# Softmax weights scaled in place before they are turned, instead of a factor tile after the product with the values

## The chip, the cores and the metric

The kernel runs on one core of one Trainium2 chip. A core has a matrix engine (TensorE, PE in the profile; its weight loads are PEld), VectorE (DVE), ScalarE (ACT), GpSimd (POOL) and SyncE (SP, which here only issues transfers). Each engine works through its own queue in order, and waits on semaphores for the others. The metric is the device time of one execution in microseconds (us); lower is better.

## The reference

One step of a one-layer hybrid decoder for two groups of tokens that share the weights: a prompt of 512 tokens and a sample group of 8 sequences with 8 new tokens each and 2048 tokens of cached past. A token row is normed and modulated, projected to queries, keys, values and gates, and goes through two attentions in parallel: a forgetting attention (8 heads, 2 key/value heads) and a native sparse attention (8 heads in 2 groups) with three branches, compressed, selected and window. Their outputs are projected, merged by gates, and a squared-ReLU MLP follows. The change touches only the prompt's attention:

```python
def fox_attend(q, cq, q_pos, k, v, ck, k_pos):
    s = einsum('btgrd,bsgd->bgrts', q, k) * HEAD_DIM ** -0.5
    p = masked_softmax(s + cq[:, None] - ck[None, :], k_pos <= q_pos)
    return einsum('bgrts,bsgd->btgrd', p, v)

def nsa_attend(...):
    p_c = masked_softmax(s_compressed, dc >= 0)
    o_c = einsum('bgrtn,bngd->btgrd', p_c, vc)
    ...
    return gates[..., 0:1] * o_c + gates[..., 1:2] * o_s + gates[..., 2:3] * o_w
```

With 512 tokens there are 8 blocks of 64 and 16 are selected, so in the prompt the selected branch reads all earlier tokens, as the window branch does; the compressed branch reads 31 compressed rows. `masked_softmax` divides the exponentials by their sum; the three branches are weighted by a gate per token, head and branch.

## The kernel before

The program has one stage after another: the sample group's compressed keys with the conditioning, the projections, the prompt's attention, the sample group's attention, the merge and output projection, the MLP. The prompt's attention lies between about 288 and 424 us of the profiled span.

It runs in 12 steps (`prompt_attention`, the loop over `steps`): a step is one branch and one head index `r`, for both groups `g` (two heads). Their order is selected 0, 1, window 0, 1, selected 2, 3, window 2, 3, then forgetting 0 to 3 (`slc`, `win`, `fox` in the names). In a step, for each group and each of the four blocks of 128 query tokens (`scores`): PE multiplies the stacked query with the key's high and low parts into a bank of PSUM; DVE subtracts the bias row and takes the row's minimum in one instruction (line 1302, tile `S`); ACT takes the exponential in place and its sum into `den`. Block `i` needs 128(i+1) columns, so a group's tile `S` has 1280 columns, and there are four such tiles. In the selected steps PE also makes the compressed scores (`cs`), and `cmp_heads` makes their softmax, already scaled by gate over sum.

The sum and the gate enter late. `scale` (line 1308) takes the reciprocal of `den`, multiplies it by the gate (not in the forgetting branch), and POOL spreads it over 64 columns per head into a tile `f` of 128x512. One step later `turn_over` (line 1318) transposes the unscaled exponentials on PE in pieces and copies them to the tiles `PT`, mostly on ACT; `factors` (line 1334) transposes `f` on PE, and ACT copies it to `F`. Another step later `weigh` (line 1343) multiplies the turned exponentials with the values into one bank (`o`), with two further products of the compressed branch into another bank (`oc`), and DVE multiplies `o` by `F` and adds.

Banks: four rotate for scores, factors and small products (`mmb`), two for transposes (`trb`), two for accumulators (`accb`: `cs`, `o`, `oc`, and the turned keys and queries).

Beside these steps others run on the same engines: the conditioning's chunks (`ada`, a product and two transposes per step, weights loaded through SP), POOL's bias rows (`bias_rows`, line 1270) and copies of the key stacks (line 1249), the sample group's selection (`sample_compare`, `sample_rank`, DVE), and from step 9 the sample group's tables (`sample_tables`, line 1556, POOL).

The order of the instructions on each engine is made by a planner that simulates a timeline with costs of its own; `link` (line 93) lets `weigh` and the first turn follow a given PE instruction by hand, and `issue_after` holds the sample group's side work behind the last minimum of its step.

## Time and profile before

| what | value |
|---|---|
| median of 3 runs | 1143.32 us (1142.42 to 1147.64) |
| the profiled execution's own time | 1140.26 us |
| its span (first to last instruction) | 1138.6 us |
| PE busy in the span | 1114.6 us, 98% |
| DVE busy | 763.3 us, 67% |
| ACT busy | 576.9 us, 51% |
| POOL busy | 316.0 us, 28% |
| granted PE clock | full |

A row of a group reads: line of the kernel, engine, operation, written tile <- read tiles, shape written <- shape read, count, then busy time in us, mean ns of one, and the idle time of the engine just before with what ended it. Tile names leave out numbers: `Sslc` is the score tile of any selected step. A piece of a chain reads: start in us, length, engine, tile, line, count. A row of waits reads: engine, tile and line that waited, what released it, us in total, times, longest.

### The profile page before, as it was taken

The page shows a single profiled execution, that of the slowest core. Times are in us where ns is not written, and L with a number is a line of the kernel's source. Part 1 is how long each engine was busy: PE and PEld are TensorE (multiplying, and loading weights), DVE is VectorE, ACT ScalarE, POOL GpSimd, SP SyncE. Part 2 cuts the span into 40 slices and gives each one's busy share as a digit, 9 for nine tenths or more (in the row PEclk, how much of TensorE's full clock was granted, in tenths as well). Part 3 has the DMA queues.
Part 4 walks back from the last instruction along what each step waited for, and adds up shares of the span by engine and source line. Part 5 has one row for each costly group of instructions (what it writes and reads, how often), then busy time and mean ns, then how long its engine had stood idle before and what let it go on. Part 6 is the DMA issues. An engine that isn't in the chain of part 4 may idle for free.

```text
span 1138.6 us, 25281 instructions
## 1 busy us (share of the span) xinstructions
PE 1114.6 (98%) x9530; PEld 968.2 (85%) x9530; DVE 763.3 (67%) x1812; ACT 576.9 (51%) x1101; POOL 316.0 (28%) x395
## 2 busy tenths in 40 slices
PE   8999999999999999999999999999999999999998
PEld 5997889999666666777999999889999998888887
DVE  3556586586798856666654446668767654898686
ACT  1465453443877774555433323356566655565420
POOL 4414320000321170001766672002564511101000
PEclk9999999999999999999999999999999999999999
DMA  9998455796586588999999986356454637877732
GB/s 232 244 279 245 132 157 203 251 329 208 179 280 203 176 298 287 309 306 298 241 268 299 317 270 224 107 159 193 152 156 137 195 116 262 312 262 256 244 104 83
DMA packets 188188, 255.52 MB, mean 224 GB/s; under 512 B 23161, under 2 KB 144706, under 8 KB 185890
## 3 DMA queue, kind: packets, MB, share of 16 engines
q1 hardware_dynamic: 148770, 173.03, 49.1%
q0 software_dynamic: 21296, 67.38, 18.3%
q10 hardware_dynamic: 18000, 13.50, 4.0%
q8 instruction: 75, 1.23, 0.4%
q14 instruction: 47, 0.39, 0.1%
HBM read 217.64 MB, written 57.12 MB: 241 GB/s over the span
## 4 chain that ended last, share of the span: by engine, by line
PE 82%; DVE 7%; DMA 6%; SPq 2%; ACT 2%; issue 2%; ACTq 0%; DVEq 0%
PE dn L83 14%; PE mg L83 9%; PE z L83 6%; PE br L83 4%; PE wo L83 4%; PE up L83 3%; DMA cpg<-in_cache_nsa_kv 3%; PE hid L83 3%; PE k L89 3%; PE ss L83 2%; DMA winr<-in_w_in 2%; PE so L83 2%; PE dns L83 2%; SPq L168 2%; PE ct L89 2%
## 5 line engine op out<-in xcount | busy, mean ns | idle before, releaser
L83 PE MATMUL z<-winh,h 128*128 128x264 f32 (+1 forms) x576 | 110.0, 286 | 1.3 <-ACT kcT L118 0.9
L83 PEld LDWEIGHTS z<-winh,h 128*128 128x128 f32 x576 | 91.4, 190 | 3.0 <-ACT kcT L118 1.3
L83 PE MATMUL z<-winl,h 128*128 128x264 f32 (+1 forms) x320 | 88.0, 284 | 0.4 <-DVE winl L137 0.4
L83 PE MATMUL mg<-hH,wmh 128*128 128x288 f32 x240 | 70.5, 295 | 0.0
L83 PE MATMUL mg<-hH,wml 128*128 128x288 f32 x240 | 70.2, 294 | 0.0
L83 PE MATMUL mg<-hL,wmh 128*128 128x288 f32 x240 | 68.4, 295 | 0.0
L83 PE MATMUL hid<-x,w1raw 128*128 128x128 f32 (+1 forms) x384 | 64.2, 310 | 0.2 <-ACT x L118 0.2
L83 PEld LDWEIGHTS z<-winl,h 128*128 128x128 f32 x320 | 60.6, 190 | 0.6 <-DVE winl L137 0.6
L118 ACT ACTIVATE x<-ct 128x512 f32<-128x512 f32 x64 | 36.4, 595 | 46.1 <-PE ct L89 31.8
L83 PEld LDWEIGHTS hid<-x,w1raw 128*128 128x128 f32 x384 | 54.2, 191 | 3.0 <-ACT x L118 0.5
L137 DVE TENSOR_TENSOR wml<-wmr,wmh 128x1024 fp32r<-128x1024 f32 x14 | 20.6, 1473 | 38.8 <-ACT wmh L118 38.8
L83 PEld LDWEIGHTS mg<-hH,wmh 128*128 128x128 f32 x240 | 45.1, 188 | 0.1
L83 PEld LDWEIGHTS mg<-hH,wml 128*128 128x128 f32 x240 | 45.0, 188 | 0.0
L83 PEld LDWEIGHTS mg<-hL,wmh 128*128 128x128 f32 x240 | 44.3, 188 | 0.0
L137 DVE TENSOR_TENSOR wp<-sums,wp 128x1024 fp32r<-128x1024 f32 x26 | 36.6, 1412 | 9.8 <-ACT wp L118 9.3
L137 DVE TENSOR_TENSOR wp<-pu,wp 128x512 fp32r<-128x512 f32 (+1 forms) x26 | 30.9, 1193 | 18.1 <-ACT wp L118 18.1
L2099 POOL TENSOR_TENSOR td<-td 128x512 f32<-128x512 f32 x24 | 34.9, 1457 | 19.4 <-DMA td<-in_w_down 19.2
L118 ACT ACTIVATE u<-u 128x1152 f32<-128x1152 f32 x29 | 33.6, 1160 | 11.7 <-DVE u L106 11.1
L89 PE MATMUL ct<-identF,ro 128*128 128x128 f32 x256 | 36.2, 275 | 3.2 <-DVE ro L121 3.2
L2099 POOL TENSOR_TENSOR td<-td,td 128x512 f32<-128x512 f32 x24 | 33.9, 1412 | 16.1 <-DMA td<-in_w_down 15.4
L118 ACT ACTIVATE mgt<-mg 128x288 f32<-128x288 f32 x32 | 12.5, 408 | 50.3 <-PE mg L83 50.3
L83 PE MATMUL br<-oL,wbh 128*128 128x288 f32 x128 | 37.8, 295 | 0.0
(1182 smaller groups left out, 3584.0 us busy)
## 6 DMA issues: line engine op xcount, KB each, us to landing
adw<-in_w_ada SPq DMA_DIRECT2D x16, 1024.0 KB
foxD<-in_cache_fox_kv SPq DMA_DIRECT2D x128, 128.0 KB
rows<-in_cache_nsa_kv SPq DMA_DIRECT2D x128, 128.0 KB
rows<-foxD SPq DMA_DIRECT2D x26, 512.0 KB
pu<-in_w_up SPq DMA_DIRECT2D x26, 512.0 KB
wdr<-in_w_down SPq DMA_DIRECT2D x26, 512.0 KB
cpg<-in_cache_nsa_kv SPq DMA_DIRECT2D x96, 128.0 KB
td<-in_w_down POOLq DMA_DIRECT2D x24, 512.0 KB, 6.5
```

Source lines behind the costliest of these rows:

```text
L83: ins = self.nc.tensor.matmul(out, a, b, start=start, stop=stop, skip_group_check=True)
L89: ins = self.nc.tensor.transpose(out, in_, self.identF[:n, :n])
L118: return self.nc.scalar.activation(out, in_, f, **kw)
L137: self.splits.append((eng or self.nc.vector).tensor_tensor(l, x, h.bitcast(F32), op=OP.subtract).ins)
L168: self.issued[eng] = getattr(self.nc, eng).dma_start(out, in_).ins
L2099: self.nc.gpsimd.tensor_tensor(out, x, y, op=OP.subtract)
```

## The change

The weights are normalised before they are turned. `scale` is called for each group as soon as that group's scores are issued: DVE takes the reciprocal of the group's four sums, and the four blocks of the tile `S` are multiplied in place by it (and by the gate, as a second per-row scalar, in the selected and window branches). Group 0 does this on POOL, group 1 on DVE. The tile `f`, its transposes and the tile `F` are gone, and so is the multiplication of the result.

The compressed values are written as a 128x128 block-diagonal matrix (zeros elsewhere), and the turned compressed weights get zeros in rows 64 to 127, so that one product with all 128 rows adds both groups' compressed results into the bank `o`. The selected result is copied out by ACT, the window result is added by DVE from the bank, the forgetting result is copied out by DVE.

`den` is laid out by group, the hand-set order of `weigh` starts from the last score product (`scored`) instead of the last product, and the scratch tag `ev` has one buffer instead of five.

```diff
--- before.py
+++ after.py
@@ -1006,7 +1006,8 @@
 
         nc = self.nc
         self.khc = pk.tile([P, 2, 2, 32], F32R, name="khc")
-        self.pvc = pk.tile([64, P], F32, name="pvc")
+        self.pvc = pk.tile([P, P], F32, name="pvc")
+        nc.gpsimd.memset(self.pvc, 0.0)
         self.pxT = []
         for kv in range(2):
             tb = self.trb(f"pct{kv}")
@@ -1075,7 +1076,8 @@
         vb = self.mmb("pvcb")
         for e in range(2):
             self.mm(vb[32 * e:32 * e + 32, 0:P], self.identF[:32, :32], self.pvs, True, True)
-        self.cp(self.pvc, vb[:64, 0:P])
+        for e in range(2):
+            self.cp(self.pvc[32 * e:32 * e + 32, 64 * e:64 * e + 64], vb[32 * e:32 * e + 32, 64 * e:64 * e + 64])
 
 
     OFF = [0, 128, 384, 768, 1280]
@@ -1085,7 +1087,7 @@
 
         self.kpos = pn.tile([P, SEQ], F32, name="kpos")
         self.iota(self.kpos, [[1, SEQ]], base=P - SEQ)
-        late = pn.tile([P, SEQ], F32, tag="ev", bufs=5, name="late")
+        late = pn.tile([P, SEQ], F32, tag="ev", bufs=1, name="late")
         self.ts(late, self.kpos, self.prow, NEG, OP.is_gt, OP.mult)
         self.tt(self.kpos, self.kpos, late, OP.add)
         rows = {("nsa", r): self.bias_rows(pp, r) for r in range(2)}
@@ -1097,6 +1099,7 @@
         self.iota(cneg, [[P, 4], [-16, 32]], base=-31, mult=1)
         gp.tensor_scalar(cneg, cneg, 0.0, NEG, op0=OP.is_lt, op1=OP.mult)
         self.tt(self.cpos, self.cpos, cneg, OP.add)
+        gp.memset(cm[64:128, 1280:1792], 0.0)
 
         kst = {"slc": self.kslc}
         qs = {("nsa", 0): self.qnsa}
@@ -1106,7 +1109,7 @@
         for n, (br, r) in enumerate(steps + [(None, None)] * 2):
             back = []
             if prev:
-                pE, pF, pbr, pr, pw = prev
+                pE, pbr, pr, pw = prev
                 T = [[], []]
 
                 def turn(g, *ks):
@@ -1120,13 +1123,14 @@
                     self.cpb = self.accb(f"cs{r}")
                 kind = "fox" if br == "fox" else "nsa"
                 q, row = qs[kind, rp], rows[kind, r]
-                den = self.small.tile([P, 4, 2], F32, tag="den", bufs=3, name=f"den{br}{r}")
+                den = self.small.tile([P, 2, 4], F32, tag="den", bufs=3, name=f"den{br}{r}")
                 tiles = [self.scores(pp, br, r, g, q[g, e], kst[br][g], row[g], den) for g in range(2)]
                 for i in range(4):
                     tiles[0][1](i)
+                self.scale(br, r, 0, tiles[0][0], den)
             if held:
-                self.chain = self.last_mm.name if br else ""
-                self.weigh(pn, *held)
+                self.chain = self.scored if br else ""
+                self.weigh(*held)
                 held = None
                 for f in back[:1]:
                     f()
@@ -1142,9 +1146,8 @@
                         self.chain = self.last_tr.name
                     tiles[1][1](i)
                     self.chain = None
-                F, cw = self.scale(pn, br, r, den), None
-                if br == "slc":
-                    cw = self.cmp_heads(pn, r)
+                self.scale(br, r, 1, tiles[1][0], den)
+                cw = self.cmp_heads(pn, r) if br == "slc" else None
             for f in back[2:]:
                 f()
             if br:
@@ -1152,13 +1155,11 @@
             if br:
                 self.ada_later()
             if prev:
-                pf = self.factors(pn, f"{pbr}{pr}", pF)
-            if prev:
-                held = pbr, pr, T, pf, pw
+                held = pbr, pr, T, pw
             prev = None
             if br is None:
                 continue
-            prev = ([t[0] for t in tiles], F, br, r, cw)
+            prev = ([t[0] for t in tiles], br, r, cw)
             if n == 0:
                 kst["win"] = self.kstack(self.pr, "win", C_WK)
                 self.oT = self.keep.tile([P, 8, NT], F32, tag="r1", bufs=1, name="oT")
@@ -1295,25 +1296,28 @@
             self.mm(pb[:, 0:n], q[:, P * i:P * i + P], kl[:, 0:n], False, br != "fox")
             if br == "fox":
                 self.mm(pb[:, n - P:n], self.identB, self.diagB, False, True)
+            self.scored = self.last_mm.name
             if br == "slc":
                 self.mm(self.cpb[:, 256 * g + 64 * i:256 * g + 64 * i + 64], q[:, P * i:P * i + P],
                         self.khc[:, g].rearrange("p a n -> p (a n)"), True, True)
 
             self.last_min = nc.vector.tensor_tensor_reduce(S, pb[:, 0:n], row[:, 0:n] if br == "fox" else row[:, SEQ - n:SEQ],
                                                            -1.0, -LOW, OP.add, OP.min, nm[:, i:i + 1]).ins
-            self.last_soft = self.act(S, S, AF.Exp, bias=nm[:, i:i + 1], scale=-1.0, accum_out=den[:, i, g:g + 1]).ins
+            self.last_soft = self.act(S, S, AF.Exp, bias=nm[:, i:i + 1], scale=-1.0, accum_out=den[:, g, i:i + 1]).ins
 
         return E, tile
 
-    def scale(self, pn, br, r, den):
-
-        self.nc.vector.reciprocal(den, den)
-        if br != "fox":
-            c = 3 * r + (1 if br == "slc" else 2)
-            self.tt(den, den, self.gate[:, 0:4, c:c + 13:12], OP.mult)
-        f = pn.tile([P, SEQ], F32, tag="ev", bufs=5, name=f"f{br}{r}")
-        self.nc.gpsimd.tensor_copy(f.rearrange("p (i g d) -> p i g d", i=4, g=2), den[:, :, :, None].to_broadcast([P, 4, 2, 64]))
-        return f
+    def scale(self, br, r, g, E, den):
+
+        self.nc.vector.reciprocal(den[:, g], den[:, g])
+        c = 12 * g + 3 * r + (1 if br == "slc" else 2)
+        eng = self.nc.vector if g else self.nc.gpsimd
+        for i in range(4):
+            S = E[:, self.OFF[i]:self.OFF[i + 1]]
+            if br == "fox":
+                eng.tensor_scalar(S, S, den[:, g, i:i + 1], None, op0=OP.mult)
+            else:
+                eng.tensor_scalar(S, S, den[:, g, i:i + 1], self.gate[:, i, c:c + 1], op0=OP.mult, op1=OP.mult)
 
     def turn_over(self, pp, br, r, g, E, ks):
 
@@ -1331,39 +1335,24 @@
             self.act(t[:, 0:o], tb[:, 0:o])
         return T
 
-    def factors(self, pn, u, den):
-
-        tb = self.mmb(f"fc{u}")
-        for i in range(4):
-            self.tr(tb[:, P * i:P * i + P], den[:, P * i:P * i + P])
-        F = pn.tile([P, SEQ], F32, tag="ev", bufs=5, name=f"F{u}")
-        self.act(F, tb)
-        return F
-
-    def weigh(self, pn, br, r, T, F, cw):
-
-        u = f"{br}{r}"
+    def weigh(self, br, r, T, cw):
+
+        out = self.oT[:, r + (0 if br == "fox" else 4), 0:SEQ]
         if br == "slc":
             cT = self.cmp_turn(r, cw)
-        out = self.oT[:, r + (0 if br == "fox" else 4), 0:SEQ]
-        ob = self.accb(f"o{u}")
+        ob = self.accb(f"o{br}{r}")
         cv = {"slc": C_SV, "win": C_WV, "fox": C_FV}[br]
         for k in range(4):
             for g in range(2):
-                self.mm(ob[64 * g:64 * g + 64, P * k:SEQ], self.zc(cv + 64 * g, 64)[:, k], T[g][k], k == 0, k == 3)
+                self.mm(ob[64 * g:64 * g + 64, P * k:SEQ], self.zc(cv + 64 * g, 64)[:, k], T[g][k], k == 0,
+                        k == 3 and br != "slc")
         if br == "slc":
-            cb = self.accb(f"oc{r}")
-            for g in range(2):
-                self.mm(cb[64 * g:64 * g + 64, :], self.pvc[32 * g:32 * g + 32, 64 * g:64 * g + 64],
-                        cT[32 * g:32 * g + 32, :], True, True)
-        if br == "win":
-            W = pn.tile([P, SEQ], F32, tag="ev", bufs=5, name=f"W{u}")
-            self.tt(W, ob, F, OP.mult)
-            self.tt(out, out, W, OP.add)
+            self.mm(ob, self.pvc, cT, False, True)
+            self.act(out, ob)
+        elif br == "win":
+            self.tt(out, ob, out, OP.add)
         else:
-            self.tt(out, ob, F, OP.mult)
-        if br == "slc":
-            self.tt(out, cb, out, OP.add)
+            self.cp(out, ob)
 
     def cmp_heads(self, pp, r):
 
@@ -1391,8 +1380,8 @@
         tb = self.mmb(f"ct{r}")
         for i in range(4):
             self.tr(tb[:64, P * i:P * i + P], w[:, i].rearrange("p g n -> p (g n)"))
-        T = self.cm[0:64, 1280:1792]
-        self.copy(T, tb[:64, :])
+        T = self.cm[:, 1280:1792]
+        self.copy(T[:64], tb[:64, :])
         return T
 
 
@@ -1522,7 +1511,7 @@
     def sample_gates(self, pn):
 
         nc, gate, Tm, Eb = self.nc, self.gate, self.Tm, self.Eb
-        self.scr, self.cut = pn.tile([P, SEQ], F32, tag="ev", bufs=5, name="gscr"), 0
+        self.scr, self.cut = pn.tile([P, SEQ], F32, tag="ev", bufs=1, name="gscr"), 0
         self.GA = self.small.tile([P, 4, 2], F32, tag="GA", bufs=1, name="GA")
         self.GB = self.small.tile([P, 2, 4], F32, tag="GB", bufs=1, name="GB")
         nc.vector.memset(self.GA[0:64], 1.0)
```

## The prediction

> **What bounds the kernel now.** I read the page first, then the busy times by stretch of the prompt's attention (288 to 424 us of the span), then the chain of waits in each stretch.
>
> ```profile
> span 1138.6 us, 25281 instructions
> ...
> PE 1114.6 (98%) x9530; PEld 968.2 (85%) x9530; DVE 763.3 (67%) x1812; ACT 576.9 (51%) x1101; POOL 316.0 (28%) x395
> ```
>
> TensorE (PE) fills the span, but its ends are modelled, so the stage has to be read with its other engines. Columns below: stretch, length, then busy us of PE, PEld, DVE, ACT, POOL, then granted clock, DMA share, GB/s.
>
> ```profile
> 288.00:304.00 16.00, 15.09 (x128) 10.71 (x121) 15.39 (x62) 13.50 (x43) 6.78 (x8) 1.00 0.45 147
> 304.00:359.00 55.00, 54.42 (x425) 37.31 (x426) 46.49 (x167) 41.95 (x117) 12.61 (x14) 1.00 0.78 261
> 359.00:398.00 39.00, 36.58 (x280) 24.45 (x279) 33.63 (x102) 29.63 (x84) 5.61 (x17) 1.00 0.56 174
> 398.00:424.00 26.00, 25.37 (x198) 17.40 (x195) 16.06 (x60) 21.88 (x60) 22.23 (x50) 1.00 0.88 296
> ```
>
> Four regimes. In 288:304 VectorE (DVE) has 0.6 us free of 16. In 304:359 and 398:424 PE hardly idles. In 359:398 PE idles 2.4 us and DVE leads the chain; POOL is loaded (22.2 of 26 us) only in the last stretch. The chain's shares for 359:398, and pieces of the whole stage's chain (start, length, engine, tile, line):
>
> ```profile
> by line: DVE qstfox L115 15.5%; PE owin L83 13.5%; DVE Swin L1302 12.8%; PE sfox L83 7.6%; issue 6.3%; DVE Sfox L1302 5.6%; DVE rank L106 5.2%; PE ptfox L89 4.3%; PE oc L83 2.8%; DVE Dt L1483 2.6%; DVE PTwin L121 2.4%; PE ptwin L89 2.3%; DV
> ```
> ```profile
> 297.68 5.10 DMA adw<-in_w_ada
> ...
> 309.42 1.00 PE oc L83 x4
> ...
> 315.48 0.59 PE fcslc L89 x4
> ...
> 345.80 0.91 PE ptslc L89 x7
> ...
> 398.13 0.44 PE fcfox L89 x4
> ```
>
> **The change part by part.** *Removed with the factor tiles*, in each of the 12 steps: four transposes on PE, one eviction on ACT, one broadcast copy on POOL, and one or two 128x512 products on DVE.
>
> ```profile
> L89 PE MATMUL fcfox<-identF,ffox 128*128 128x128 f32 x16 | 2.4, 272 | 0.0
> L118 ACT ACTIVATE Ffox<-fcfox 128x512 f32<-128x512 f32 x4 | 2.3, 586 | 0.0
> L1315 POOL COPY ffox<-denfox 128x512 f32<-128x512 f32 x4 | 2.5, 618 | 12.4 <-DMA browfox<-cumD 10.8 <-DVE denfox L1310 1.5
> L106 DVE TENSOR_TENSOR oT<-oc,oT 128x512 f32<-128x512 f32 x4 | 2.8, 692 | 1.1 <-PE oc L83 1.0
> L106 DVE TENSOR_TENSOR Wwin<-owin,Fwin 128x512 f32<-128x512 f32 x4 | 2.8, 692 | 6.4 <-PE owin L83 6.4
> L106 DVE TENSOR_TENSOR denwin<-denwin,gate 128x8 f32<-128x8 f32 x4 | 0.7, 168 | 0.0
> L1310 DVE RECIPROCAL denwin<-denwin 128x8 f32<-128x8 f32 x4 | 0.8, 193 | 0.0
> ```
>
> On PE the group of four costs 0.44 us on the chain (398.13), 0.59 where its load starts cold (315.48). All 12 make 12 x 0.44 = 5.3 us. Where PE leads, that is path: the groups of five steps fall in 304:359 and of four in 398:424 with its end, so 9 x 0.44 = **-4.0 us**. The three in the DVE-led stretch I count at nothing; at most they are another -1.3. ACT loses 12 x 0.59 and gets four copies of the selected result back; it is nowhere the chain's leader, so nothing, between 0 and -1.
>
> *Added on DVE*: the four in-place scalings of group 1 (128, 256, 384 and 512 columns, 1280 in all) and a second reciprocal.
>
> ```profile
> L112 DVE TENSOR_SCALAR late<-kpos,prow 128x512 f32<-128x512 f32 x1 | 0.5, 472 | 0.0
> ...
> L112 DVE TENSOR_SCALAR maps<-maps 128x64 f32<-128x64 f32 x6 | 1.4, 305 | 0.0
> ```
> ```profile
> L110 DVE TENSOR_SCALAR nsq<-x,nrs 128x1024 f32<-128x1024 f32 x3 | 2.2, 745 | 0.0
> ```
>
> One per-row scalar: 472 ns at 512 columns and 745 at 1024 give 0.533 ns a column and 199 ns fixed. The forgetting branch (one scalar) costs 4 x 0.199 + 1280 x 0.000533 = 1.48 us a step. With two scalars, the 64-column row is 305 against 199 + 34 = 233, so 0.07 more each: 1.77 us for selected and window. The reciprocal (0.19) about cancels the gate's product (0.17) there, and adds 0.19 in forgetting. Against that go the products: selected -1.38 a step, window -0.69, forgetting 0 (a copy replaces the product). Over 12 steps: 8 x 1.80 + 4 x 1.67 - 4 x 1.38 - 4 x 0.69 = 14.4 + 6.7 - 5.5 - 2.8 = +12.8 us of DVE, placed as +1.8 in 288:304, +3.5 in 304:359, +2.5 in 359:398, +5.0 in 398:424. The second and fourth stretch have 8.5 and 9.9 us of DVE free: nothing. In 359:398 DVE goes from 33.6 to 36.1 of 39 and leads the chain: **+2.0**, between 0 (it takes its own 5.4 us of gaps) and +2.5. In 288:304 the 1.8 us meets 0.6 free, but PE's order there holds the conditioning product until its weights land at 302.78 (297.68 + 5.10), which covers late turns until then: **+1.0**, between 0 and +3.
>
> The added reciprocal of group 0 waits for ACT's last sum of that group; behind it on DVE stand group 1's minima, and behind those PE's score banks. The planner can put it after them, since its reader, POOL, has time (below); I count nothing. No transfer is added or moved, SP's queue is as before.
>
> *Added on POOL*: the four scalings of group 0. Behind them in POOL's queue stand the next bias rows and the copies of the key stacks. That operation on POOL:
>
> ```profile
> L1632 POOL TENSOR_SCALAR scr<-scr 128x512 f32<-128x512 f32 x2 | 3.3, 1656 | 0.1
> ...
> L1599 POOL TENSOR_SCALAR scr<-scr,t_row 128x512 f32<-128x512 f32 x1 | 2.0, 2017 | 0.1
> ...
> L1600 POOL TENSOR_SCALAR scr<-scr,slope_i 128x512 f32<-128x512 f32 x1 | 0.7, 700 | 0.0
> ...
> L1618 POOL TENSOR_SCALAR scr<-scr 128x1 f32<-128x1 f32 x2 | 0.5, 268 | 0.1
> L1585 POOL TENSOR_SCALAR scr<-scr,t_row 128x64 f32<-128x64 f32 x1 | 0.5, 519 | 0.1
> L1576 POOL TENSOR_SCALAR scr<-scr,prow 128x32 f32<-128x32 f32 x1 | 0.4, 398 | 0.0
> ```
>
> One scalar in place: 398 ns at 32 and 1656 at 512 columns give 2.62 ns a column and 0.31 fixed, so 4 x 0.31 + 1280 x 0.00262 = 4.6 us a step. Two operations show both ends: a comparison and a product (519 at 64, 2017 at 512) would make 5.5 us, a sum and a product (268 at one column, 700 at 512) 2.2 us. I take 4.6 for all, as the forgetting branch has exactly the first form, and keep 2.2 to 5.5. The Trainium skill, GPSIMD Engine Reference, section 4.1 (Engine selection), holds that one-input work on this engine runs near line rate; by that these steps would be the 2.2 us end, and the row of 1656 ns disagrees.
>
> Who waits for it? The first turn of a step is one step later. For the third selected step:
>
> ```profile
> 333.62 0.19 ACT L118 ACTIVATION_READ_ACCUMULATOR Sslc<-Sslc,nmslc 128x1 f32 x1
> ```
>
> Group 0's last sum is there at 333.8, its turn ran at 345.8: 12 us for about 5 us of work, so nothing. Without that cover a step would cost up to 4.6. In 398:424, however, POOL's 22.2 us becomes 22.2 - 3 x 0.6 + 3 x 4.6 = 34.2 of 26, so the sample group's tables, which share the queue, slide about 8 us. They end at 421.8 and are first read at 435.3, and two window loads are issued behind them on POOL:
>
> ```profile
> L1632 POOL TENSOR_SCALAR scr<-scr x2: 1592/1656/1719, 414.3 to 420.1; 128x512 f32<-128x512 f32 x2
> ```
> ```profile
> 435.29 0.68 DVE L1831 CUSTOM_DVE_ANT_0 sS<-ss,scr 128x512 f32<-128x512 f32 x1
> ```
>
> That leaves 13.5 us of room: nothing, as long as the scalings go ahead of the tables.
>
> *One product for the compressed values*: now four records of 128x512 in 1.00 us (309.42). Afterwards two records that use all rows; the nearest row is
>
> ```profile
> L83 PE MATMUL selx<-Dt 128*32 128x512 f32 x2 | 1.0, 604 | 0.0
> ```
>
> so also 1.0: nothing, from 0 to -0.5. It takes one accumulator bank less, of which there are two. Waits on those banks:
>
> ```profile
> PE owin L83 <- DVE qstfox L115: 0.9, 1, 0.9
> ...
> PE oc L83 <- DVE qstfox L115: 0.4, 1, 0.4
> ```
>
> The second goes: **-0.4**. The two clears, the narrower copies of the compressed values and the smaller scratch are under 1 us on engines with room.
>
> Sum: -4.0 + 2.0 + 1.0 - 0.4 = -1.4 us. The profiled execution took 1140.26 us, 1.66 over its span; the shown runs' median, 1143.32, is 3.06 above it. So 1138.9 by the profile and **1142** in runs.
>
> **The rivals.** *All of it arrives* (0.20): DVE packs without loss and all 12 groups count, with 0.9 for those that started cold: -5.3 - 0.9 - 0.4 = -6.6, so 1136.7. For it: DVE's gaps exceed its addition in every stretch after 304. Against: DVE at 93% in order, in 359:398.
>
> *DVE and POOL hold each other up* (0.15). Two executions show what a meeting costs:
>
> ```profile
> L1277 POOL TENSOR_SCALAR brownsa<-kpos x6: 1488/1492/1945, 290.7 to 327.8; 128x512 f32<-128x512 f32 x6
> ```
> ```profile
> 794.24 0.69 DVE L2301 TENSOR_TENSOR sums<-sums,pu 128x512 f32<-128x512 f32 x1
> 794.96 1.68 DVE L2301 TENSOR_TENSOR sums<-pu,sums 128x512 f32<-128x512 f32 x1
> ```
>
> A meeting took 0.46 us from POOL and about 1.0 from DVE. If POOL's 4.6 us still run when DVE scales group 1, two meetings a step add 2.0 us: 359:398 has 33.6 + 2.5 + 8 = 44.1 of DVE in 39 us, plus half its gaps, +7.8; 288:304 has 15.4 + 1.8 + 4 = 21.2 in 16, +5.2; less 4.4, some +8.6, so 1152. With one meeting a step the same working gives 1145.9, no longer told from no change; it decides from there, so I price it between, 1149.5. Against: group 0 is ready about half a step earlier. The Trainium skill, SBUF — State Buffer, section "Who interferes with whom", says more: POOL and a DVE instruction of this kind share one port as an exclusive lock, and the second fully blocks. The rows above agree that the loser waits; no row shows it for a scaling.
>
> *POOL is late at the end* (0.12, slower): if the tables go first, the last step's scaling starts after 417.0 (its turn, 421.6, less 4.6) and pushes the last turns by about the 8 us excess: 1150. The turn:
>
> ```profile
> 421.61 0.92 PE ptfox L89 x7
> ```
>
> *The transfers take it back* (0.08): from 424 to 560 the DMA share is 0.92, so an earlier start need not end earlier: 1143.3.
>
> ```profile
> 424.00:560.00 136.00, 130.80 (x2604) 98.62 (x2603) 90.72 (x293) 74.65 (x167) 20.10 (x34) 1.00 0.92 293
> ```
>
> **How the numbers follow.** My forecast has 0.45. Its own range is 1137 to 1147: below, the other three groups (-1.3), no loss in 359:398 (-2.0) and at the start (-1.0), -0.5 for the one product; above, +2.0 at the start and +0.5 in 359:398, and what the planner's new order and the runs' own spread (1142.42 to 1147.64) add. About 0.5% (5.7 us) is what can be told from no change: faster is below 1137.6, slower above 1149.0. Faster: the first rival and the forecast's lower edge, 0.25. Slower: the second and third, 0.27. Same: the rest, 0.48. The range runs from the first rival's time less its cover to just past the third: 1135.5 to 1151.
>
> **What would show it.** Right: no fc groups on PE, 304:359 shorter by about 2 us, 398:424 by under 2, 359:398 longer by up to 2.5; DVE scalings near 0.20 us + 0.53 ns a column; POOL's near 1.6 us at 512. Wrong: turns that wait for POOL, DVE scalings well over 0.55 us at 512 columns, or first turns after 303 us.

## The result and the profile after

The changed kernel takes **1156.84 us** (median of 6 runs, 1151.12 to 1160.49) against 1143.76 for the kernel before on the same chip (6 runs, 1141.42 to 1147.64): ratio 1.0109, 95% interval 1.0081 to 1.0137. It is slower, by 13.1 us in the medians, and outside the predicted range. The profiled execution took 1155.96 us.

The profile's page of the changed kernel, the span and the busy line:

```profile
span 1154.3 us, 25215 instructions
...
PE 1122.4 (97%) x9474; PEld 967.9 (84%) x9474; DVE 777.1 (67%) x1853; ACT 572.6 (50%) x1093; POOL 344.3 (30%) x433
```

The same stretches as in the prediction (length, then busy us of PE, PEld, DVE, ACT, POOL, then granted clock, DMA share, GB/s):

```profile
288.00:304.00 16.00, 14.15 (x106) 10.06 (x106) 14.32 (x55) 12.21 (x38) 10.46 (x14) 1.00 0.47 147
304.00:359.00 55.00, 53.60 (x419) 36.48 (x418) 50.04 (x184) 41.40 (x118) 21.92 (x29) 1.00 0.81 257
359.00:398.00 39.00, 33.35 (x235) 21.49 (x235) 33.68 (x105) 27.47 (x75) 9.65 (x13) 0.95 0.59 173
398.00:424.00 26.00, 25.36 (x166) 15.59 (x163) 17.01 (x61) 18.18 (x51) 22.90 (x35) 0.95 0.74 234
```

The factor groups are gone, DVE is fuller in 304:359, and yet PE is less busy in 359:398 than before (33.35 against 36.58 us), and the granted clock, full in all four stretches before, is 0.95 in two of them. A yardstick for all runs below is the **stage**, from the end of the last projection product (`z`) to the end of the last forgetting product (`ofox`): 287.57 to 429.44 = 141.9 us before, 288.81 to 443.23 = 154.4 us after. Of the 15.7 us between the two profiled executions, 12.5 are lost here, 1.2 ahead of it and 1.9 behind it. The last rows of `ofox`, before and after (start, us, engine, line, what):

```profile
428.58 0.86 PE L83 MATMUL ofox<-PTfox,zF 128*64 128x256 f32 x6
```
```profile
442.37 0.86 PE L83 MATMUL ofox<-PTfox,zF 128*64 128x256 f32 x6
```

The waits of PE within it, after the change (engine, tile and line that waited, releaser: us in all, times, longest):

```profile
PE oslc L83 <- DVE qstfox L115: 2.7, 1, 2.7
PE owin L83 <- DVE qstfox L115: 2.2, 1, 2.2
PE gts L83 <- DVE gscr L106: 1.9, 1, 1.9
PE sslc L83 <- DVE nmslc L1304: 1.8, 5, 0.4
PE xsuf L83 <- POOL fscr L741: 1.6, 1, 1.6
```

**The first two.** The first wait on DVE's timeline (start, us, engine, line, what), before and then after:

```profile
365.30 0.42 DVE L1302 CUSTOM_DVE_ANT_0 Swin<-swin,brownsa 128x256 f32<-128x256 f32 x1
...
365.85 1.53 DVE L115 SCALAR_TENSOR_TENSOR qstfox<-qfox,gcol,qstfox 64x512 fp32r<-64x512 f32 x2
```
```profile
367.30 0.42 DVE L1304 CUSTOM_DVE_ANT_0 Swin<-swin,brownsa 128x256 f32<-128x256 f32 x1
...
367.74 1.51 DVE L1320 TENSOR_SCALAR Swin<-Swin,denwin,gate 128x128 f32<-128x128 f32 x4
369.16 0.55 DVE L1304 CUSTOM_DVE_ANT_0 Swin<-swin,brownsa 128x384 f32<-128x384 f32 x1
...
369.75 1.53 DVE L115 SCALAR_TENSOR_TENSOR qstfox<-qfox,gcol,qstfox 64x512 fp32r<-64x512 f32 x2
```

The forgetting query stack `qfox` is turned in one of the two accumulator banks, which is free only once DVE has read it (`qstfox`). Before, that read came 0.1 us behind the minimum of 256 columns; now four scalings and another minimum stand between, and PE, whose next product needs the bank, stands still.

**The last two.** POOL's last sum, the DVE copy that stands ahead of what PE's `gts` waits for, and PE's `xsuf`, before the change:

```profile
412.11 0.32 POOL L741 TENSOR_TENSOR fscr<-fscr 128x64 f32<-128x64 f32 x1
```
```profile
417.30 0.11 DVE L121 COPY gscr<-Eb 64x8 f32<-64x8 f32 x1
```
```profile
418.00 0.43 PE L83 MATMUL xsuf<-fscr 128*128 128x64 f32 x2
```

After it, POOL's queue and the same copy:

```profile
419.96 4.30 POOL L1318 TENSOR_SCALAR Sfox<-Sfox,denfox 128x128 f32<-128x128 f32 x4 [0.95 <-DVE denfox L1312]
...
424.79 0.58 POOL L1578 TENSOR_TENSOR scr<-nbf,scr 64x64 f32<-64x64 f32 x2
425.34 1.25 POOL L1590 TENSOR_TENSOR scr<-scr 128x512 f32<-128x512 f32 x1
...
430.16 0.40 POOL L741 TENSOR_TENSOR fscr<-fscr 128x64 f32<-128x64 f32 x1
```
```profile
424.77 1.85 DVE L121 COPY gscr<-Eb 64x8 f32<-64x8 f32 x1
```

The sum `fscr` of the sample group, which POOL had ready at 412.43, is ready at 430.56, and the product `xsuf` that reads it stands ahead of the third forgetting weighing in PE's order. The copy of 64x8 took 0.11 us before and 1.85 here, just while POOL ran a row of two-input operations. The Trainium skill, SBUF — State Buffer, section "Who interferes with whom", has a copy on DVE in its two-port mode and POOL excluding each other for the whole instruction. This row fits that a copy waits for POOL, but it outlasts every single POOL operation beside it (the longest took 1.25 us), and the order of the starts does not prove it.

**The clock.** Windows of 3.4 us around three of the waits (columns as above):

```profile
366.60:370.00 3.40, 1.28 (x9) 0.85 (x8) 3.37 (x14) 3.14 (x9) 0.00 (x0) 1.00 0.67 202
370.00:373.40 3.40, 2.84 (x8) 1.01 (x10) 2.89 (x6) 1.96 (x5) 0.15 (x1) 0.51 0.90 285
...
393.90:397.30 3.40, 1.31 (x10) 0.81 (x8) 3.37 (x14) 2.73 (x8) 0.00 (x0) 1.00 0.25 69
397.30:400.70 3.40, 3.08 (x10) 1.04 (x12) 1.26 (x5) 1.03 (x4) 1.18 (x2) 0.51 0.55 145
...
424.70:428.10 3.40, 1.34 (x21) 0.90 (x19) 3.29 (x9) 1.25 (x6) 3.22 (x11) 0.99 0.89 285
428.10:431.50 3.40, 1.81 (x11) 1.28 (x10) 2.29 (x9) 0.96 (x2) 2.87 (x9) 0.50 0.87 284
431.50:434.90 3.40, 3.40 (x12) 1.18 (x12) 2.05 (x8) 1.13 (x4) 3.25 (x9) 0.50 0.36 122
```

A window in which PE worked 1.3 us is followed by one at half the granted clock, twice in a row at the end. PE worked 2.84 + 3.08 + 1.81 + 3.40 = 11.1 us in these, which full speed does in half: 5.6 us. The Trainium skill, TensorE: Matmul & The Clock Gate, Part 1, has the clock halve after an idle window of about 3.4 us. The length agrees; the condition is milder here, as these windows were not idle.

The profile is no exception in this: the mean granted clock is 0.991 to 0.994 in all six executions of the change, and 0.995 to 1.0, with a median of 0.999, in the 93 of the kernel before that ran beside the experiments.

The four waits (8.4, less the 1.3 us of waits on `qstfox` before) and the clock (5.6) make 12.7 us; less what the removal brings in the stage (1.8, first experiment below) 10.9 of the 12.5. The wait of `sslc`, 1.8 us in five pieces against 0.3 before, is about the rest.

### The profile page after: what moved, and what is told of

It reads as the page before. It is cut to its first block, busy times and chain, and to the rows that moved or that the text cites. A ratio compares the mean times of both kernels' runs of the same rounds, so it can differ in the third digit from the quotient of the medians.

```text
span 1154.3 us, 25215 instructions
## 1 busy us (share of the span) xinstructions
PE 1122.4 (97%) x9474; PEld 967.9 (84%) x9474; DVE 777.1 (67%) x1853; ACT 572.6 (50%) x1093; POOL 344.3 (30%) x433
## 4 chain that ended last, share of the span: by engine, by line
PE 74%; DMA 9%; DVE 8%; ACT 3%; SPq 3%; issue 2%; POOL 1%; ACTq 0%; DVEq 0%; POOLq 0%
PE dn L83 14%; PE z L83 8%; PE mg L83 8%; DMA cpg<-in_cache_nsa_kv 4%; PE br L83 4%; PE wo L83 3%; PE up L83 3%; SPq L168 2%; PE hid L83 2%; PE k L89 2%; PE dns L83 2%; PE ss L83 2%; PE so L83 1%; PE oslc L83 1%; DMA rows<-foxD 1%
## 5 line engine op out<-in xcount | busy, mean ns | idle before, releaser
L89 PE MATMUL k<-identF,rows 128*128 128x128 f32 x256 | 36.2, 281 | 2.2 <-DVE kt L121 1.0
L118 ACT ACTIVATE mgt<-mg 128x288 f32<-128x288 f32 x32 | 12.5, 407 | 51.4 <-PE mg L83 51.3
L2088 POOL TENSOR_TENSOR td<-td 128x512 f32<-128x512 f32 x24 | 31.6, 1320 | 20.6 <-DMA td<-in_w_down 20.3
```

The source lines that it names most:

```text
L89: ins = self.nc.tensor.transpose(out, in_, self.identF[:n, :n])
L118: return self.nc.scalar.activation(out, in_, f, **kw)
L2088: self.nc.gpsimd.tensor_tensor(out, x, y, op=OP.subtract)
```

## The experiments

All times are medians beside runs of the kernel before on the same chip; the interval is that of the ratio to it.

| run | us | ratio, 95% | stage us | half clock in the stage, us |
|---|---|---|---|---|
| the change | 1156.84 | 1.0081 to 1.0137 | 154.4 | 13.7 |
| e9 no scaling | 1143.49 | 0.9974 to 1.0035 | 140.0 | 0 |
| e10 DVE's only | 1155.03 | 1.0046 to 1.0106 | 148.9 | 6.8 |
| e11 POOL's only | 1152.16 | 1.0045 to 1.0101 | 147.8 | 6.8 |
| e5 before + DVE by 1 | 1155.77 | 1.0073 to 1.0180 | 154.5 | 10.2 |
| e6 before + POOL by 1 | 1153.16 | 1.0051 to 1.0098 | 151.3 | 6.8 |
| e7 before + one product | 1145.50 | 1.0000 to 1.0046 | 146.5 | 3.4 |
| e1 stacks' bank | 1150.12 | 1.0037 to 1.0071 | 147.3 | 6.8 |
| e14 DVE's only, stacks' bank | 1149.58 | 1.0038 to 1.0085 | not read | not read |
| e12 before, stacks' bank | 1143.71 | 0.9976 to 1.0023 | 142.4 | 0 |
| e13 POOL's only, not the last three | 1147.41 | 1.0011 to 1.0058 | 141.7 | 0 |
| e3 dummies on PE | 1152.68 | 1.0053 to 1.0108 | 150.4 | 3.4 |
| e2 xsuf last | 1161.01 | 1.0109 to 1.0186 | 154.1 | 13.7 |
| e4 group 0 on ACT | 1158.46 | 1.0091 to 1.0168 | 153.4 | 6.8 |
| e16 stacks' bank, tail on ACT | 1156.44 | 1.0091 to 1.0163 | 150.6 | 13.7 |
| e15 two scalars | 1156.04 | 1.0084 to 1.0158 | 147.5 | 6.8 |
| e8 stacks' bank, two scalars, dummies | 1152.74 | 1.0051 to 1.0094 | 146.1 | 6.8 |
| e17 stacks' bank, two scalars | 1147.63 | 1.0004 to 1.0059 | 142.3 | 0 |
| e18 before + unused column | 1147.45 | 1.0000 to 1.0051 | 141.8 | 0 |

The time is from 4 to 10 executions, the stage from one profiled execution each (that of e14 took 1162.48 us and is not read). That one lies 6.7 us above its run's median in e1, 4.8 to 5.0 above it in e6, e7 and e9, and 4.9 below it in e8, so the two columns of a row need not fit each other.

**What each part is worth.** The scalings of group 0, of group 1 or of both left out of the changed kernel (e9 both; e10 and e11 with `(0,)` and `(1,)`):

```diff
-        for i in range(4):
+        for i in range(0 if g in (0, 1) else 4):
             S = E[:, self.OFF[i]:self.OFF[i + 1]]
```

> The changed kernel with all 96 in-place scalings left out (group 0's on POOL and group 1's on DVE), so the exponentials go unnormalised into their turns and the branches are not weighted right; the reciprocals stay. What is left is what the change removes, and the one product. By the prediction's own terms: PE -4.0 to -5.3, DVE 8.3 us less, so 1138 to 1140. If the two parts that were measured on the kernel before (+12.2 on DVE, +9.6 on POOL) simply add up to the change's +13.1, the removal must be worth -8.7 or more: 1133 to 1136. If removal is worth nothing, 1142 to 1145, and the additions do not add up.

> The changed kernel with group 0's scalings on POOL left out (group 0 goes unnormalised), group 1's on DVE kept. My theory, amended (DVE's in-order scalings ahead of minima and of qstfox lengthen the PE-DVE ping-pong in 359:398; the waits on qstfox stay, with their half clock; the end place goes): 1147 to 1151. Rival 1 (POOL is the whole cause): as without any scaling. Rival 2 (DVE alone): 1155 to 1158, as the changed kernel.

> The changed kernel with group 1's scalings on DVE left out (group 1 goes unnormalised), group 0's on POOL kept. My theory, amended: POOL's backlog costs at the end only (xsuf <- POOL fscr and the half clock behind it), 5 to 8 us over the kernel without scalings: 1143 to 1148. Rival 1 (POOL): 1155 to 1158. Rival 2 (DVE): as without any scaling, within 2 us.

Without any scaling the kernel is level with the one before, within 0.26% faster and 0.35% slower. In its profile the stage is 1.8 us shorter, not 4 to 5, and the next stage gives that back; PE's timeline of that kernel, with the idle time before each row:

```profile
537.24 0.33 PE L89 MATMUL k<-identF,rows 128*128 128x128 f32 x1 [0.56 <-DMA rows<-in_cache_nsa_kv]
539.85 0.68 PE L89 MATMUL k<-identF,rows 128*128 128x128 f32 x2 [2.28 <-DMA rows<-in_cache_nsa_kv]
```

Before, PE did not wait for these gathered rows. This execution took 1148.32 us, though, 4.8 over its median; what takes the 1.8 us back in the others is not shown. So no gain from the removal can be told from none, and what the scalings cost is a loss. Each engine's part costs on its own: DVE's 8.9 us of stage over e9, POOL's 7.8, both 14.4; they overlap little. Both were dearer than my theory had them (e10 by 4, e11 by 4 us over its upper edge in the medians).

Where it is lost shows in how much later than in e9 a weighing ends, counted from the start of the stage (us; e13 is POOL's part without its last three steps, below):

| end of the weighing | the change | e10 | e11 | e13 |
|---|---|---|---|---|
| third selected | 1.3 | 2.6 | 1.6 | 1.6 |
| fourth selected | 5.1 | 6.2 | 1.6 | 1.6 |
| last window | 9.0 | 9.8 | 1.6 | 1.6 |
| second forgetting | 8.7 | 9.1 | 1.0 | 1.6 |
| third forgetting | 14.4 | 8.9 | 7.7 | 1.7 |

DVE's part loses most at the two weighings that wait for `qstfox`, POOL's at the one behind `xsuf`; these three places make 3.8 + 3.9 + 5.7 = 13.4 of the change's 14.4 us.

The same two parts on the kernel before, with a constant 1 and nothing removed (e5; in e6 the same for group 0 on POOL):

```diff
                 F, cw = self.scale(pn, br, r, den), None
+                self.by_one(1, tiles[1][0])
...
+    def by_one(self, g, E):
+
+        eng = self.nc.vector if g else self.nc.gpsimd
+        for i in range(4):
+            S = E[:, self.OFF[i]:self.OFF[i + 1]]
+            eng.tensor_scalar(S, S, 1.0, None, op0=OP.mult)
```

> The kernel before, nothing removed from it, with group 1's exponentials multiplied by the constant 1 in place on DVE in each of the 12 steps (same shapes and same place as the change's scalings; about 1.25 to 1.5 us a step). Rival 2 (DVE's added work, in order ahead of the minima and of qstfox, is the cause): most of the loss returns, 1149 to 1155. Rival 1 (POOL): at most +1.5, so 1143 to 1145. My theory of PE waits behind DVE's scalings in 359:398, with a half-clock stretch: +4 to +8, so 1147.5 to 1151.5.

> The kernel before, nothing removed from it, with group 0's exponentials multiplied by the constant 1 in place on POOL in each of the 12 steps (about 4.3 us a step, the one-scalar form). Rival 1 (POOL): +8 or more, above 1151. Rival 2 (DVE): within 1 us of before. My theory: POOL's backlog costs only at the end, behind the last forgetting steps (gscr, fscr): +2 to +5, so 1145.5 to 1149.

Both losses return, and both lie over the ranges of my theory (by 4.3 and 4.2 us), without reciprocals, gates or any missing factor: it is added work in that place. The lengths are not quite those of the change: with a constant DVE's scalings took 15.4 us in all against 18.9 in the change, POOL's 48.3 against 37.5. In e6 PE waited 2.9 us for `xsuf`, and the clock halved behind it, as in the change. In e5 PE waited for `qstfox` only 0.5 us, and longest for another DVE instruction:

```profile
PE cumn L83 <- DVE pers L121: 2.0, 1, 2.0
```

So the bank of the query stacks is where DVE's work was met in the change, and not the only place where it can cost.

The second part alone, on the kernel before; the compressed weights are divided by the selected factor, so that the factor multiplies both:

```diff
+        self.tt(den, den, sden.rearrange("p i g -> p g i"), OP.mult)
         nc.vector.reciprocal(dv, dv)
...
-            cb = self.accb(f"oc{r}")
-            for g in range(2):
-                self.mm(cb[64 * g:64 * g + 64, :], self.pvc[32 * g:32 * g + 32, 64 * g:64 * g + 64],
-                        cT[32 * g:32 * g + 32, :], True, True)
+            self.mm(ob, self.pvc, cT, False, True)
```

> The kernel before with its factor tiles, its scalings after the weighing and everything else kept, and only the second part of the change: the compressed values as one product into the selected branch's bank. For that the compressed weights are divided by the selected branch's factor (one small product on DVE, 128x8, more, and one 128x512 sum less in each of four steps: 4 x (0.69 - 0.17) = 2.1 us less DVE; one accumulator bank less). All theories: no loss from this part, 1141 to 1144. If it is above 1145.5, the one product costs something that none of them names.

The time lies between no change and +0.46%, 1.5 us over the range that I gave: at best nothing. Its profile, of an execution 5.0 us above the median, shows a half-clock stretch at 371.9. Whether this part costs a little or nothing stays open.

**The bank.** The changed kernel (e1), e10 (e14) and the kernel before (e12) with the forgetting query stacks in the scores' four banks:

```diff
             if n == 6:
+                self.stackb = self.mmb
                 qs["fox", 0] = self.qstack(self.pkq, "fox", C_FQ, 0, 0)
```

> The changed kernel, but the two forgetting query stacks are turned in the scores' banks instead of the accumulators' two. My theory (new waits on PE, each followed by a stretch at half the granted clock): the two waits PE oslc <- DVE qstfox 2.7 us and PE owin <- DVE qstfox 2.2 us go, and the half-clock stretches at 370.0 and 397.3 with them (3.4 us each, worth 1.7 each), together up to 8.3 us; up to 3 us may come back, as the stacks now take score banks. So 1148.5 to 1152, against 1156.8 for the changed kernel. Rival 1 (POOL's scalings are what costs, by their length): unchanged, 1155 to 1158. Rival 2 (DVE's 12.8 us of added work cost as such): unchanged as well.

> The kernel of the DVE-only run (group 0 left unnormalised) with the forgetting query stacks in the scores' banks. If DVE's cost is that its scalings stand ahead of qstfox while PE waits for the accumulator bank (2.5 and 2.0 us, each followed by 3.4 us at half clock), 4.5 + 3.4 less up to 2 come back: 1147 to 1150. If DVE's 17 us cost as such, 1153 to 1156 stays.

> The kernel before, with nothing but the forgetting query stacks turned in the scores' banks, a candidate to beat both kernels. There the waits on qstfox are 0.9 and 0.4 us and no stretch is at half clock, so the mend can be worth 1.3 us at most, and the stacks now take score banks: 1141.5 to 1144.5. If these banks were worth 5 us or more by themselves (not through DVE's scalings in front of qstfox), it would be below 1139.

6.7 us come back in the change and 5.5 with DVE's scalings alone, none in the kernel before: the bank matters because of what stands ahead of its reader. Of what DVE's scalings cost in time (1155.03 - 1143.49 = 11.5 us) that is about half; the rest stays with DVE's longer queue. In e1's profile (an execution of 1156.77 us, 6.7 above the median) a wait for the same reader is left, on a score bank, and with it one long half-clock stretch:

```profile
PE ct L89 <- DVE qstfox L115: 1.5, 1, 1.5
```

**POOL's place.** e11 with the last three forgetting steps left out as well:

```diff
-        for i in range(0 if g in (1,) else 4):
+        for i in range(0 if g in (1,) or (br, r) in (("fox", 1), ("fox", 2), ("fox", 3)) else 4):
```

> The kernel of the POOL-only run with the last three forgetting steps' scalings on POOL left out as well (nine of 12 steps keep theirs; group 1 and those three go unnormalised). If POOL's cost is its backlog at the end (gscr, fscr, xsuf, and the half clock behind them), it is gone: 1142 to 1146. If POOL's scalings cost in every step (late turns, meetings with DVE), 1149 to 1152 stays.

The stage is 141.7 us long, so three of the twelve steps carry most of what POOL costs in it: 147.8 - 141.7 = 6.1 us. The other 1.7 over e9 are there from the first two selected weighings on. In the medians the three steps make 1152.16 - 1147.41 = 4.8 of POOL's 8.7 us over e9. The median came 1.4 us over what I expected, and the profiled execution (1144.34 us) is the only one of the ten at full clock; from e9 (1143.49) the nine other steps can't be told apart surely. What ended the longest wait in e11:

```profile
PE xsuf L83 <- POOL fscr L741: 3.1, 1, 3.1
```

**The clock.** The change with dummy products of identities on PE, ten ahead of the weighings in steps 7 and 9 and six ahead of `xsuf`:

```diff
+                if n in (7, 9):
+                    self.cmp_warm(10)
                 self.weigh(*held)
...
+                self.chain = self.last_tr.name
+                self.cmp_warm(6)
                 self.forget_sums()
+                self.chain = None
```

> The changed kernel with dummy products on PE of identities, ten ahead of the weighing of the last selected step, ten ahead of that of the last window step and six ahead of xsuf: every wait stays as it is, PE only idles less in it. If the granted clock halves because PE idles (my theory), the windows at 370.0, 397.3 and 428.1 stay at full speed: 1.7 + 1.7 + 3.4 = 6.8 us at most, less what the dummies overhang, so 1150 to 1153. If the clock is only a bystander, 1156 to 1160.

PE waits as long or does useless work instead, yet 4.2 us come back, and the three stretches run at full clock (a new one at half came at 299.4):

```profile
369.40:372.80 3.40, 3.40 (x24) 1.91 (x21) 1.88 (x5) 1.91 (x4) 1.19 (x3) 1.00 0.64 219
394.00:397.40 3.40, 3.09 (x24) 1.76 (x24) 1.93 (x6) 1.27 (x4) 0.94 (x2) 1.00 0.44 136
426.00:429.40 3.40, 2.65 (x18) 1.36 (x18) 1.66 (x8) 0.82 (x3) 3.06 (x10) 1.00 0.49 166
```

By this run about a third of the loss was the clock, which only follows the waits.

**Three misses.** `xsuf` behind the last step (e2), group 0 on ACT in all steps (e4), and the same with the condition `br == "fox" and r and not g`, that is in the last three forgetting steps only, with the stacks' bank (e16):

```diff
-            if n == 11:
-                self.forget_sums()
+        self.forget_sums()
```
```diff
+            if not g:
+                if br != "fox":
+                    self.tt(den[:, 0], den[:, 0], self.gate[:, 0:4, c], OP.mult)
+                for i in range(4):
+                    S = E[:, self.OFF[i]:self.OFF[i + 1]]
+                    self.act(S, S, scale=den[:, 0, i:i + 1])
+                return
```

> The changed kernel, but the product xsuf of the sample group's forgetting sums is issued after the last step instead of ahead of the next to last weighing, so that PE does not stand in order behind POOL's chain of sums. My theory: the wait PE xsuf <- POOL fscr 1.6 us goes, and one of the two half-clock windows at 428.1 (1.7 us): 1153 to 1155. Rival 1 (POOL by its length): the last scaling is no earlier, so at most 1 us, 1155.5 to 1157. Rival 2 (DVE's work): no change.

> The changed kernel with group 0 scaled on ACT instead of POOL (per-row scale of an activation, after a small product of the reciprocal with the gate on DVE). POOL is left with less than before the change. My theory: what goes is the third place only (PE gts <- DVE gscr 1.9 us, PE xsuf <- POOL fscr 1.6, half clock 428.1 to 434.9, 3.4 us) and DVE's meetings with POOL; the two waits on qstfox stay, as DVE's scaling of group 1 still stands ahead of them. 1148 to 1151. Rival 1 (POOL is the whole cause): 1141 to 1144. Rival 2 (DVE's added work is): 1154 to 1158.

> The changed kernel computing all it should, with two mends: the forgetting query stacks in the scores' banks, and group 0 of the last three forgetting steps scaled on ACT instead of POOL, so that POOL's sums for xsuf start on time. My theory: 1150.1 of the first experiment less xsuf's 0.9 and what the end still lost, so 1145 to 1149, no better than before, since the kernel without any scalings was only level with it. If below 1142, the end alone was the cause and the mended change wins.

Moving `xsuf` took its wait away but left the one on `gts` and the half clock at 427.0, and the time rose, by its profile behind the stage. Moving POOL's work to ACT removed POOL's waits and made new ones of the same size; in e4 (in e16 the last of these is 2.7):

```profile
PE oslc L83 <- DVE qstfox L115: 3.4, 1, 3.4
PE swin L83 <- DVE nmwin L1304: 2.2, 1, 2.2
PE ncnt L83 <- ACT PTfox L118: 1.9, 1, 1.9
```

None of the engines that were tried had room at the places that count, ACT neither, though it is busy half of the span.

**The length on POOL.** In the profile of the change the two-scalar form is the faster one:

```profile
L1318 POOL TENSOR_SCALAR Sfox<-Sfox,denfox 128x512 f32<-128x512 f32 x4 | 6.3, 1565 | 0.0
...
L1320 POOL TENSOR_SCALAR Swin<-Swin,denwin,gate 128x512 f32<-128x512 f32 x4 | 3.1, 774 | 0.0
```

So group 0's forgetting scalings on POOL were given a second scalar of ones: in a tile of its own (e15; e8 with the stacks' bank and ten dummies), then from a tile that exists (e17, with the stacks' bank), and the added tile alone on the kernel before (e18):

```diff
             if br == "fox":
-                eng.tensor_scalar(S, S, den[:, g, i:i + 1], None, op0=OP.mult)
+                if g:
+                    eng.tensor_scalar(S, S, den[:, g, i:i + 1], None, op0=OP.mult)
+                else:
+                    eng.tensor_scalar(S, S, den[:, g, i:i + 1], self.ones[:, 0:1], op0=OP.mult, op1=OP.mult)
```
```diff
+        self.unit = self.small.tile([P, 1], F32, tag="unit", bufs=1, name="unit")
+        gp.memset(self.unit, 1.0)
```

> The changed kernel with nothing but group 0's forgetting scalings on POOL in the two-scalar form (second scalar a column of ones): by the profile of the changed kernel 2.4 us a step against 4.3, so some 7.6 us less of POOL in the last four steps. My theory (backlog at the end): part of gts' 1.9 and xsuf's 1.6 us and one half-clock window (1.7) go: 1152 to 1155. If only the number of instructions on POOL counts, 1156 to 1158.

> The changed kernel with three mends: the forgetting query stacks in the scores' banks (as in the first experiment), group 0's forgetting scalings on POOL in the two-scalar form (second scalar a column of ones; the selected and window scalings of that form took 2.4 us a step against 4.3), and ten dummy products ahead of the weighing of the last selected step, where the first experiment still showed a wait and 6.8 us at half clock. My theory: 1150.1 less 3.4 for the clock and 0 to 2 for xsuf, so 1144.5 to 1147.5, no better than before. Rival 1 (POOL's length): 12 to 8 us less POOL in the last steps makes more of it, below 1144. Rival 2 (DVE): as the first experiment, 1149 to 1151.

> The changed kernel with the two mends that shortened its stage, the forgetting query stacks in the scores' banks and group 0's forgetting scalings on POOL in the two-scalar form; the second scalar is now a column of the tile of ones that the kernel has, so no tile is added. In the two earlier kernels of that form, which added a tile of one column, the products of the last stage (dn, 128x512) took 395 ns instead of 389 in the profile. If the added tile did that, they are back at 389 here, and the time is the first experiment's 1150.1 less some 1 to 3 us: 1146.5 to 1149.5. If the two-scalar form brings it, they stay at 395 and the time at 1150 to 1153.

> The kernel before with nothing but an unused tile of one column (128x1, set to 1 by POOL) added in the pool of small tiles. If that tile is what lengthens the dn products, they take 395 ns and the kernel 1147 to 1149 (some 840 products by 5 to 6 ns); if not, 389 ns and 1142 to 1145.

e15's stage is 6.9 us shorter than the change's, its time 0.8 only, over the range that I gave; e8 came 5.2 us over its range. Both have the added tile, and the last stage's products `dn` explain much of it: from the first to the last of them e15 takes 4.2 us more than the change (another 2.2 us lie ahead of the stage). The products before, then in e18:

```profile
L83 PE MATMUL dn<-wdT_0h,as 128*128 128x512 f32 x64 | 19.5, 389 | 0.0
```
```profile
L83 PE MATMUL dn<-wdT_0h,as 128*128 128x512 f32 x64 | 19.9, 395 | 0.0
```

With one unused column of 4 bytes a partition they are 6 ns longer. The kernel before is 3.7 us slower with it in the medians, 0 to 0.51% by the interval; its profile, 195.3 us from the first to the last of them against 191.4, agrees. In e17, without that tile, they are at 389 and the stage is back to 142.3 us with the clock full in all of it:

```profile
359.00:398.00 39.00, 35.03 (x265) 22.93 (x262) 35.98 (x113) 28.86 (x79) 10.11 (x16) 1.00 0.62 185
398.00:424.00 26.00, 25.75 (x186) 16.47 (x186) 21.70 (x80) 21.59 (x60) 24.28 (x55) 1.00 0.83 273
```

It is the best form of the change, 9.2 us faster than as made, and still 0.04 to 0.59% slower than the kernel before, for which its profile has no row in this stage; that execution and one other of the ten had a mean clock of 0.999, the eight others 0.992 to 0.997. None of these kernels beats that one, and e9 says why: with all the scalings for nothing the change would only be level.

## Why the prediction was wrong, step by step

- *PE, "nine of 12 groups ... -4.0 us"*: failed in size. The groups are gone, but the stage without scalings is 1.8 us shorter in its one profile, and no gain is left in the medians. In that profile a wait for gathered rows takes it back, as the rival "the transfers take it back" has it (0.08); for other executions that is not shown.
- *DVE in 359:398, "+2.0, between 0 and +2.5"*: failed, the largest of the errors. The rows for the scaling were right (1.51 us for four, predicted 1.77; 1.25 to 1.74 for the forgetting form, predicted 1.48). The step that failed is the one from busy time to cost: I took the added 2.5 us as the most that the work could cost there, and let DVE's gaps take part of it. e10's stage is 8.9 us over e9's, 7.2 of it between the third selected and the last window weighing. DVE's largest gap of that stretch before, the 2.71 us here, was DVE waiting for PE, and work put ahead of a reader that PE waits for lengthens both:

```profile
382.17 0.69 DVE L106 TENSOR_TENSOR Wwin<-owin,Fwin 128x512 f32<-128x512 f32 x1 [2.71 <-PE owin L83]
```

- *"The second goes: -0.4"*: failed in sign. I counted the one bank saved and not the reader of the other, `qstfox`, behind which DVE's scalings put 4.9 us of waits instead of 1.3.
- *The added reciprocal, nothing*: not contradicted. DVE's in-order waits for ACT's sums (rows below) are 2.8 us in the change, on DVE and not on PE, and e5, which has no added reciprocal, loses as much as e10.

```profile
DVE denslc L1312 <- ACT Sslc L118: 1.5, 1, 1.5
...
DVE denfox L1312 <- ACT Sfox L118: 1.3, 3, 0.8
```

- *POOL, 4.6 us a step, "That leaves 13.5 us of room: nothing"*: the price held for the forgetting form (4.30 us for four) and was half of that for the other (0.77 us at 512 columns), whose sum lies near the lower bound of 2.2. The room was wrong: I took the tables' first reader at 435.3, and the first reader in that queue is `xsuf`, 418.00 before. POOL's end cost 6.1 us of the stage and 4.8 in the medians (e11 against e13). The rival "POOL is late at the end" was right on the place, with the wrong reader.
- *Start, +1.0 (0 to 3)*: stands, near its upper edge. First turns came at 303.2, just past the bound that I gave, in a stage that starts 1.2 us later. The conditioning's product behind them came 2.1 us later than before, 0.8 without that shift, and held by DVE and no longer by its weights (rows below, before and after); the first weighing ended 2.9 us later, counted from the stage's start.

```profile
302.92 1.07 PE L83 MATMUL ada<-adw 128*32 128x256 f32 x16 [0.48 <-DMA adw<-in_w_ada]
```
```profile
304.97 1.07 PE L83 MATMUL ada<-adw 128*32 128x256 f32 x16 [0.60 <-DVE nmslc L1304]
```

- *One product, 0*: 3.36 us for the 18 products in the change's chain of waits against 2.30 and 1.00 before, so 0.06 more; e7 leaves 0 to +0.46% in time.

```profile
325.32 3.36 PE oslc L83 x18
```
```profile
320.80 2.30 PE oslc L83 x16
323.10 1.00 PE oc L83 x4
```

- *No term for the clock*: missing altogether, 5.6 us by the windows, 4.2 by e3. No row of the prompt's attention before has less than full clock, so the trace gave no price; but a range built on idle time that is paid once was too narrow.
- *The rival "DVE and POOL hold each other up" (0.15)*: small. Group 1's scalings took 18.9 us of DVE in the change and 17.9 without POOL's (e10), group 0's 37.5 of POOL and 37.3 without DVE's (e11); the copy of 1.85 us, with the wait on `gts` behind it, is the one such meeting behind which PE is seen to wait.
- *The rivals as alternatives*: POOL's late end and, in part, DVE and POOL in each other's way came true together, on top of DVE's loss. Separate chances for mechanisms that can add up make the range too short on the side on which they all lie.

## What to carry to other kernels

Before work is put into another engine's gaps, ask what ended each gap: where it was the engine that now has to wait, the gap is no room. For every instruction added to an in-order queue, list the next readers behind it up to the one that holds a bank or stands in front of the leading engine's order; POOL's tail here had such a reader 17 us ahead of the one I looked at. And price a removed cost by leaving it out: one run without the scalings would have shown that there was no gain to tell from none.

## What the runs showed that I had not expected

- *The clock needs no idle window.* Windows of 3.4 us in which PE worked 1.3 us were followed by half clock, and a half-clock window with 1.81 us of work by another. Over the profiles of all runs, PE worked 0.6 to 2.3 us in the windows ahead of a drop, and other windows with 1.4 us and more were passed at full clock, so no bound can be read. By estimate a 2 us wait can thus cost up to 1.7 us more (3.4 us of work at half speed), if it falls mostly into one window.
- *POOL is faster with two per-row scalars than with one*: 774 against 1565 ns at 128x512. No run here shows why.
- *A tile of 4 bytes a partition that nothing reads* lengthened the last stage's products from 389 to 395 ns. That it shifts the addresses of tiles behind it is argued, not shown; but an experiment that adds a tile should look at stages it doesn't touch.
